# Seven block products for eight in the gate and up projections of a decoder trunk's FFNs, and narrower FFN chunks

## The chip, the core and the metric

The kernel runs on one core of a Trainium2 chip. The metric is the device time in microseconds, the median of the runs shown; smaller is better. TensorE is the matrix engine (PE in the rows; PEld is its weight load), VectorE is DVE, ScalarE is ACT, GpSimd is POOL, and SP issues the DMAs.

## What is computed

One step of a decoder trunk of two layers over 576 tokens: 512 of a prompt and 8 sequences of 8. Each layer has a half-step FFN, a mixer of three gated branches and a second FFN, each behind an RMSNorm with a per-sequence shift and scale. The FFN is what is changed here:

```python
def _swiglu(h, w_gu, w_dn):
    a, b = jnp.split(h @ w_gu, 2, axis=-1)
    return (jax.nn.silu(a) * b) @ w_dn
...
x = x + 0.5 * mod[:, 0, 2][:, None, :] * _swiglu(h, w1_gu, w1_dn)
```

The model width is 1024 (eight blocks of 128), the FFN width 2816 (22 blocks of 128), all in float32. `mod`, the modulation, is `silu(c) @ w_ada + b_ada`, nine vectors of 1024 a layer.

## The kernel before

Everything lies transposed in SBUF: channels on the partitions, tokens along the row. The 576 tokens are two halves of 288 columns (256 of the prompt, 32 of the samples).

**Products.** Every float32 operand is kept as a high and a low part, and a product is three matmuls of 128x128 by 288 columns: low weight by high input (L288), high by low (L290), high by high (L291). `units` (L278) does this for the k blocks of one output tile (128 output channels, one half of the tokens) in one PSUM bank of five, and calls a function that reads the bank. `pair` (L539) runs two output tiles for both halves, 2 x 2 x 8 x 3 = 96 matmuls in a gate or up product.

**Weights.** A raw tile holds 256 output columns of a matrix, 1 MB; SP loads it (L123) into one of two buffers. `Weights.split` (L203) cuts it into slots of 128x1024, a high and a low part each, six slots in all (`NHL`): the high part on ScalarE (L223), the low part, raw less high, on VectorE (L227); every third slot on GpSimd (L221, L225). A slot is cut when an earlier one has had its last use (`done`), so cuts run several tiles ahead of PE.

**FFN.** `ffn` (L548) goes over the width in three chunks of 8, 8 and 6 tiles. Of each chunk it makes gate and up products, two output tiles at a time (`evac_a`, Silu on ScalarE, L556; `evac_b`, the product on VectorE L566 and its two parts on ScalarE L568 and VectorE L569), then the down products over the chunk's tiles, added into `x` (`xupd`, L458). An FFN's first two gate and two up tiles lie in `start_stage` (L479), interleaved with the RMSNorm of the second half of the tokens (`norm3`, L416); the end of a stage (`end_stage`, L509) interleaves the first half's.

**Modulation.** The matmuls for the later modulation vectors are spread as 64 steps over the two FFNs of layer 0, a step every three units; `sched_ada` (L1349) loads each step's four tiles (1 MB) two steps ahead, and `ada_mm` (L319) runs it.

All this is written in program order: each engine's instructions run in the order in which the code issues them, and an engine waits at an instruction until its inputs are there and its output is free.

## Time and profile before

| | before |
|---|---|
| median of three runs | 2694.2 us (2693.83 to 2694.84) |
| span of the profiled execution | 2692.9 us (the page gives no other time of it) |
| TensorE busy (matmuls) | 2668.0 us, 99% |
| TensorE busy (weight loads) | 2581.1 us, 96% |
| VectorE busy | 1043.0 us, 39% |
| ScalarE busy | 631.8 us, 23% |
| GpSimd busy | 603.7 us, 22% |
| read from and written to HBM | 288.02 MB and 3.25 MB |

The page gives each engine's busy time over the whole span. A matmul's record reaches from its start to its modelled end, and matmuls overlap, so the price of one is the distance of two starts. An engine's waits, the chain of work that ended last, and windows of the span tell where its share of idle time lies.

### The profile page before, as it was taken

The numbers are of one execution on the slowest core, as the hardware profiler recorded it, in microseconds if no ns is written. First come the engines' busy times: TensorE is split into PE (matmuls) and PEld (weight loads), VectorE is DVE, ScalarE is ACT, GpSimd is POOL, SyncE is SP. The second block draws the span as 40 slices with busy tenths as digits, with TensorE's granted clock in tenths as the row PEclk, the third lists the DMA queues.
The fourth block names the chain that finished last, engine by engine and source line by source line (L and its number), as shares of the span: only waits on it lengthen the run. The fifth ranks groups of instructions, "written<-read, shape, count | busy, mean of one in ns | idle before, by whom it ended". The sixth has DMA issues, their size and how long they took to land.

```text
span 2692.9 us, 46258 instructions
## 1 busy us (share of the span) xinstructions
PE 2668.0 (99%) x20040; PEld 2581.1 (96%) x20040; DVE 1043.0 (39%) x2094; ACT 631.8 (23%) x1167; POOL 603.7 (22%) x520
## 2 busy tenths in 40 slices
PE   8999999999999999999999999999999999999998
PEld 5999999999999999989999999999999999999998
DVE  5232232643325633223253323237333456232324
ACT  4211112331223321121232122124212233212122
POOL 2111112502133421121142111223020523211111
PEclk9999999999999999999999999999999999999999
DMA  9544542322222254545213222222222232222221
GB/s 287 204 164 166 176 132 69 99 78 79 87 83 83 95 195 165 187 142 172 67 59 110 94 79 79 80 90 85 80 79 93 77 95 68 94 79 85 89 67 56
DMA packets 259689, 294.03 MB, mean 109 GB/s; under 512 B 9996, under 2 KB 223292, under 8 KB 259470
## 3 DMA queue, kind: packets, MB, share of 16 engines
q1 hardware_dynamic: 259486, 291.08, 32.8%
q8 instruction: 158, 2.59, 0.4%
q14 instruction: 45, 0.37, 0.0%
HBM read 288.02 MB, written 3.25 MB: 108 GB/s over the span
## 4 chain that ended last, share of the span: by engine, by line
PE 95%; DVE 2%; DMA 1%; POOL 1%; issue 0%; SPq 0%; ACT 0%; DVEq 0%; POOLq 0%; ACTq 0%
PE mm L288 31%; PE mm L291 30%; PE mm L290 30%; PE adab L326 2%; DVE hlo L436 1%; PE mm L297 1%; DMA adap<-in_w_ada_dram 0%; POOL accsq L373 0%; PE tpb L712 0%; DMA xin<-in_x_prompt_dram 0%; POOL wlo L225 0%; DMA ada<-in_w_ada_dram 0%; DVE u L431 0%; PE nrb L412 0%; DVE us L446 0%
## 5 line engine op out<-in xcount | busy, mean ns | idle before, releaser
L288 PE MATMUL mm<-hhi,wlo 128*128 128x288 f32 x4320 | 1281.7, 298 | 0.0
L291 PE MATMUL mm<-hhi,whi 128*128 128x288 f32 x4320 | 1272.1, 295 | 0.0
L290 PE MATMUL mm<-hlo,whi 128*128 128x288 f32 x4160 | 1229.1, 295 | 0.0
L288 PEld LDWEIGHTS mm<-hhi,wlo 128*128 128x128 f32 x4320 | 810.9, 188 | 34.6 <-issue 33.5
L291 PEld LDWEIGHTS mm<-hhi,whi 128*128 128x128 f32 x4320 | 810.9, 188 | 0.0
L290 PEld LDWEIGHTS mm<-hlo,whi 128*128 128x128 f32 x4160 | 781.1, 188 | 0.3
L227 DVE TENSOR_TENSOR wlo<-raw,whi 128x1024 fp32r<-128x1024 f32 (+1 forms) x277 | 344.3, 1245 | 656.2 <-ACT whi L223 649.2
L221 POOL TENSOR_SCALAR whi<-raw 128x1024 fp32r<-128x1024 f32 (+1 forms) x125 | 131.9, 1055 | 1588.2 <-PE mm L291 1519.0
L288 PE MATMUL mm<-ghi,wlo 128*128 128x288 f32 x1408 | 418.3, 297 | 0.0
L291 PE MATMUL mm<-ghi,whi 128*128 128x288 f32 x1408 | 414.7, 295 | 0.0
L290 PE MATMUL mm<-glo,whi 128*128 128x288 f32 x1408 | 414.5, 294 | 0.0
L223 ACT ACTIVATE whi<-raw 128x1024 fp32r<-128x1024 f32 (+1 forms) x277 | 285.5, 1034 | 517.1 <-PE mm L291 289.5
L225 POOL TENSOR_TENSOR wlo<-raw,whi 128x1024 fp32r<-128x1024 f32 (+1 forms) x125 | 308.9, 2471 | 10.4
L288 PEld LDWEIGHTS mm<-ghi,wlo 128*128 128x128 f32 x1408 | 264.1, 188 | 20.3 <-issue 20.1
L290 PEld LDWEIGHTS mm<-glo,whi 128*128 128x128 f32 x1408 | 264.1, 188 | 0.2
L291 PEld LDWEIGHTS mm<-ghi,whi 128*128 128x128 f32 x1408 | 264.1, 188 | 0.0
L462 DVE SCALAR_TENSOR_TENSOR x<-mm,mod,x 128x256 f32<-128x256 f32 x224 | 108.1, 483 | 321.6 <-PE mm L291 321.5
L568 ACT ACTIVATE ghi<-g 128x288 fp32r<-128x288 f32 x176 | 78.2, 444 | 455.8 <-DVE g L566 455.8
L566 DVE TENSOR_TENSOR g<-mm,sil 128x288 f32<-128x288 f32 x176 | 80.5, 457 | 266.5 <-PE mm L291 265.5
L556 ACT ACTIVATE sil<-mm 128x288 f32<-128x288 f32 x176 | 71.5, 411 | 430.1 <-PE mm L291 404.1
L569 DVE TENSOR_TENSOR glo<-g,ghi 128x288 fp32r<-128x288 f32 x176 | 89.9, 511 | 90.2 <-ACT ghi L568 89.7
L747 ACT ACTIVATE sil<-mm 128x288 f32<-128x288 f32 x96 | 38.8, 409 | 182.4 <-PE mm L291 167.6
(219 smaller groups left out, 1912.8 us busy)
## 6 DMA issues: line engine op xcount, KB each, us to landing
raw<-in_w_gu_dram SPq DMA_DIRECT2D x88, 1024.0 KB
ada<-in_w_ada_dram SPq DMA_DIRECT2D x256, 256.0 KB
raw<-in_w_in_dram SPq DMA_DIRECT2D x48, 1024.0 KB
raw<-in_w_dn_dram SPq DMA_DIRECT2D x32, 1024.0 KB
raw<-in_w_dn_dram SPq DMA_DIRECT2D x16, 768.0 KB
adap<-in_w_ada_dram SPq DMA_DIRECT2D x32, 256.0 KB
raw<-in_w_o_dram SPq DMA_DIRECT2D x8, 1024.0 KB
raw<-in_w_out_b_dram SPq DMA_DIRECT2D x8, 512.0 KB
```

Source lines behind the costliest of these rows:

```text
L221: nc.gpsimd.tensor_scalar(dst_v(hi), src, 1.0, 0.0, ALU.mult, ALU.add)
L223: nc.scalar.activation(dst_v(hi), src, AF.Copy)
L225: nc.gpsimd.tensor_sub(dst_v(lo), src, dst_v(hi).bitcast(F32))
L227: nc.vector.tensor_sub(dst_v(lo), src, dst_v(hi).bitcast(F32))
L288: nc.tensor.matmul(o, wlo, rhi, start=(k == 0), stop=False)
L290: nc.tensor.matmul(o, whi, rlo, start=False, stop=False)
L291: nc.tensor.matmul(o, whi, rhi, start=False, stop=(k == K - 1 and not late))
L462: nc.vector.scalar_tensor_tensor(out=xc, in0=ps[:, :PH], scalar=mod[:, gidx + m, 0:1], in1=xc, op0=ALU.mult, op1=ALU.add)
L556: nc.scalar.activation(t, ps[:, :HALF], AF.Silu)
L566: nc.vector.tensor_mul(g, ps[:, :HALF], sil.pop((j, h)))
L568: nc.scalar.activation(hi, g, AF.Copy)
L569: nc.vector.tensor_sub(glo[j][:, h * HALF:(h + 1) * HALF], g, hi.bitcast(F32))
```

## The change

**Gate and up products by blocks.** For every gate or up pair except an FFN's first, the pair's product is taken as a product of 2 x 2 blocks: the 1024 channels are two halves of four k blocks, the 256 output columns two tiles, the 576 tokens two halves. Seven block products of four k blocks stand for eight, which Strassen's algorithm allows in Winograd's form. It needs four sums of weight blocks (S1 to S4, on GpSimd, in place in the raw tile, L337), four sums of input blocks (T1 to T4, on VectorE, once an FFN, `t_sum` L649, and split by `t_split` L660 and L661), and sums of the products. `Groups.group` runs the seven products in this order: A12·B21 into a bank of its own, copied out by ScalarE (L717); the last product of the group before (`tail`); A11·B11 into the bank `ak`, added to the copy by VectorE (L723); S1·T1, copied out (L731); S2·T2 added on into `ak`, read by VectorE (L736); S4·B22, added by VectorE (L741); S3·T3 added on into `ak`, read by VectorE (L748); and A22·T4 added on into `ak`, deferred as the tail. A product into `ak` waits until the read before it is done. Three of four products of gate and up now go to GpSimd (L912).

**Cuts.** Such a raw tile is cut in eight steps, in the order a, d, S1, S3, c, S2, S4, b: slots a, b and c of 128x1024, d of 128x512, all with the high part on ScalarE (L288) and the low part on VectorE (L290). There are five slots and two half slots for six slots. `pump` runs as many further steps as a place in the group allows.

**Chunks.** The FFN's chunks are 4, 4, 4, 4 and 6 tiles in layer 0, and 4, 6, 6 and 6 in layer 1. The down products of all chunks but the last are added into `x` by three engines (L775, L776, L781).

**Start of an FFN.** The norm (`norm3t`) makes the float32 inputs as tiles of 128x576, which the T sums then overwrite. `start_stage` cuts its third slot behind the normalisation where none is left (`pay`).

**Modulation.** Steps are loaded one step ahead, and their groups go by vectors.

```diff
 NSLOT = 25
-NHL = 6
+NQ = 16
+NB = 5
+NHL = 5
+NHD = 2
+_FEW = ((0, 4), (4, 4), (8, 4), (12, 4), (16, 6))
+_MANY = ((0, 4), (4, 6), (10, 6), (16, 6))
...
+    def add_st(src, c0):
+        def dma(t):
+            nc.sync.dma_start(t.rearrange("p (k c) -> p k c", c=256),
+                              src[:, c0:c0 + 256].rearrange("(k p) c -> p k c", p=P))
+        raws.append((dma, None))
+    def add_ffn(gu, dn, chunks):
+        for f0, nf in chunks:
             for j in range(f0, f0 + nf, 2):
-                add_cols(gu, j * P, KT)
-                add_cols(gu, 2816 + j * P, KT)
+                add = (lambda src, c: add_cols(src, c, KT)) if j == 0 else add_st
+                add(gu, j * P)
+                add(gu, 2816 + j * P)
             for m in range(0, 8, 2):
                 add_cols(dn[f0 * P:(f0 + nf) * P, :], m * P, nf)
...
+                    self.steps += [(r, x) for x in ("a", "d", "S1", "S3", "c", "S2", "S4", "b")]
...
+        def can(self):
+            if self.at >= len(self.steps):
+                return False
+            r, x = self.steps[self.at]
+            if r not in self.rawt:
+                return False
+            if x == "d":
+                return len(self.free["d"]) > 0
+            return x in ("S1", "S2", "S3", "S4") or len(self.free["w"]) > 0
...
+                a11, a12, a21, a22 = first[:, 0], first[:, 1], second[:, 0], second[:, 1]
+                last = x == "b"
+                if x == "d":
+                    hi, lo = self.pair_of(True)
+                    self.cut(hi.rearrange("p (k c) -> p k c", c=P),
+                             lo.rearrange("p (k c) -> p k c", c=P), a22, "AD")
+                    self.slots[-1]["d"] = (hi, lo)
+                    filled = False
+                elif x in ("a", "b", "c"):
+                    hi, lo = self.pair_of(False)
+                    t3 = t.rearrange("p (k c) -> p k c", c=256)
+                    src = t3[:, :, P:256] if x == "c" else t3[:, :, 0:P]
+                    self.cut(hi.rearrange("p (k c) -> p k c", c=P),
+                             lo.rearrange("p (k c) -> p k c", c=P), src, "AD")
+                    if x == "a":
+                        self.slots.append({})
+                    self.slots[-1][x] = (hi, lo)
+                else:
+                    filled = False
+                    o, p, q, op = {"S1": (a22, a21, a22, ALU.add), "S3": (a21, a11, a21, ALU.subtract),
+                                   "S2": (a11, a22, a11, ALU.subtract),
+                                   "S4": (a12, a12, a11, ALU.subtract)}[x]
+                    nc.gpsimd.tensor_tensor(out=o, in0=p, in1=q, op=op)
+            if last:
                 del self.rawt[r]
...
+        def pump(self, n):
+            while n and self.can():
+                self.step()
+                n -= 1
...
+        def need(self, s, x):
+            while x not in s:
+                self.step()
+            return s[x]
...
+    def t_sum(i, q):
+        o, a, b = {1: ((0, q), (1, q), (0, q)), 3: ((1, q), (1, q + 2), (1, q)),
+                   2: ((1, q + 2), (1, q + 2), (0, q)), 4: ((0, q + 2), (0, q + 2), (1, q + 2))}[i]
+        nc.vector.tensor_sub(U[o], U[a], U[b])
...
+        nc.scalar.activation(hi, u3, AF.Copy)
+        nc.vector.tensor_sub(lo, u3, hi.bitcast(F32))
...
+    def t_early():
+        return [lambda i=i, q=q: t_sum(i, q) for i in (1, 3, 2, 4) for q in range(2)] + [
+            lambda i=i, q=q: t_split(i, q) for i in (1, 2, 3) for q in range(2)]
...
+    def blk(i):
+        if isinstance(i, str):
+            k0, h = {"11": (0, 0), "21": (4, 0), "22": (4, 1)}[i]
...
+        def product(self, bank, slot, k0, rhs, start):
+            for k in range(4):
+                whi, wlo = wk(slot, k0 + k)
+                rhi, rlo = rhs(k)
+                o = bank[:, :HALF]
+                nc.tensor.matmul(o, wlo, rhi, start=(start and k == 0), stop=False, skip_group_check=True)
+                nc.tensor.matmul(o, whi, rlo, start=False, stop=False, skip_group_check=True)
+                nc.tensor.matmul(o, whi, rhi, start=False, stop=(k == 3), skip_group_check=True)
...
+        def group(self, evac, m):
+            s = W.take()
+            out = lambda i, h: evac(m + i, h)
+            dk = balloc()
+            self.product(dk, W.need(s, "a"), 4, blk("21"), True)
+            d = qalloc("pd")
+            nc.scalar.activation(d, dk[:, :HALF], AF.Copy)
+            brelease(dk)
+            W.pump(1)
+            self.flush()
+            ak = balloc()
+            self.product(ak, s["a"], 0, blk("11"), True)
+            nc.vector.tensor_add(d, ak[:, :HALF], d)
+            out(0, 0)(d, d)
+            W.give(s["a"])
+            W.pump(1)
+            tick(1)
+            ek = balloc()
+            self.product(ek, W.need(s, "c"), 4, blk(1), True)
+            e = qalloc("pe")
+            nc.scalar.activation(e, ek[:, :HALF], AF.Copy)
+            brelease(ek)
+            W.pump(2)
+            self.product(ak, W.need(s, "b"), 0, blk(2), False)
+            u = qalloc("pu")
+            nc.vector.tensor_add(u, ak[:, :HALF], e)
+            W.pump(1)
+            tick(1)
+            fk = balloc()
+            self.product(fk, s["b"], 4, blk("22"), True)
+            nc.vector.tensor_add(u, fk[:, :HALF], u)
+            brelease(fk)
+            out(0, 1)(u, u)
+            W.give(s["b"])
+            W.pump(1)
+            tick(1)
+            self.product(ak, s["c"], 0, blk(3), False)
+            nc.vector.tensor_add(e, ak[:, :HALF], e)
+            out(1, 1)(e, e)
+            W.give(s["c"])
+            W.pump(1)
+            def tail():
+                self.product(ak, W.need(s, "d"), 0, blk(4), False)
+                out(1, 0)(ak, None)
+                brelease(ak)
+                W.give(s["d"])
+                W.pump(1)
+                tick(1)
+            self.tail = tail
...
+            if late:
+                t = qalloc("xt")
+                nc.scalar.activation(t[:, :PH], ps[:, :PH], AF.Copy, scale=mod[:, gidx + m, 0:1])
+                nc.vector.tensor_mul(
+                    t[:, PH:].rearrange("p (s t) -> p s t", s=4),
+                    ps[:, PH:HALF].rearrange("p (s t) -> p s t", s=4),
+                    mod[:, gidx + m, 1 + 4 * h:5 + 4 * h].unsqueeze(2).to_broadcast([P, 4, 8]))
+                xc = x[:, m, c0:c0 + HALF]
+                nc.gpsimd.tensor_add(xc, xc, t)
...
+        nb = norm_bc(1, nrmbank())
+        late_lo.extend(norm3t(1, l, sub, nb) if st else norm3(1, l, sub, us[0], nb))
+        if W.taken >= len(W.slots):
+            W.pay(None, 1)
         s.append(W.take())
...
+        todo = t_early() if st else []
...
+        units([(s[i], 0, KT, hk(1), evac(i, 1)) for i in (0, 1)], {k: lambda: some(1) for k in range(KT)},
+              True)
...
+                g = sil.pop((j, h))
+                (nc.vector if own is None else nc.gpsimd).tensor_mul(g, ps[:, :HALF], g)
...
-        for f0, nf in ((0, 8), (8, 8), (16, 6)):
+        chunks = CHUNKS[l][sub // 2]
+        for f0, nf in chunks:
...
-                    pair(KT, hk, evac_a, j)
-                    pair(KT, hk, evac_b, j)
+                    G.group(evac_a, j)
+                    G.group(evac_b, j)
...
+            xu = lambda m, h: xupd(m, h, gidx, False, True)
+            if f0 + nf < 22:
+                pair4(nf, grhs, xu, 0, G.flush)
+                for m in range(2, 8, 2):
+                    pair(nf, grhs, xu, m)
...
-    def sched_ada(g0, g1, start, every):
...
-        for n, s in enumerate(steps):
-            def fn(s=s, n=n):
-                ada_mm(s)
-                if n + 2 < len(steps):
-                    ada_fetch(steps[n + 2])
...
+    def sched_ada(groups, start):
+        steps = [(vecs, i, every) for vecs, every in groups for i in range(4 * len(vecs))]
+        ada_fetch(steps[0][:2])
+        at = start
+        for n, (vecs, i, every) in enumerate(steps):
+            def fn(n=n, vecs=vecs, i=i):
+                ada_mm((vecs, i))
+                if n + 1 < len(steps):
+                    ada_fetch(steps[n + 1][:2])
+                if i == 4 * len(vecs) - 1:
+                    after(1, lambda: ada_fin(vecs))
+            after(at, fn)
+            at += every
...
+    after(4, lambda: sched_ada((((2,), 2), ((3, 4), 3), ((5, 6), 3), ((7, 8), 3)), 1))
...
+    after(3, lambda: sched_ada((((9, 10), 3), ((11, 12), 3), ((13, 14), 3), ((15, 16), 3), ((17,), 3)), 2))
```

**VectorE in the gate and up products of layer 1, one pair and the next.** Before; `wlo` is the low part of a weight slot, `g` the product of gate and up, `glo` its low part:

```order
L566 TENSOR_TENSOR g_2113_14981<-mm_14954,sil_14861 128x288
L569 TENSOR_TENSOR glo_14980<-g_2113_14981,ghi_14979 128x288
L566 TENSOR_TENSOR g_2117_15012<-mm_14985,sil_14888 128x288
L569 TENSOR_TENSOR glo_15011<-g_2117_15012,ghi_15010 128x288
L566 TENSOR_TENSOR g_2119_15041<-mm_15016,sil_14915 128x288
L569 TENSOR_TENSOR glo_14980<-g_2119_15041,ghi_14979 128x288
L227 TENSOR_TENSOR wlo_15046<-raw_14834,whi_15045 128x1024
L566 TENSOR_TENSOR g_2123_15074<-mm_15049,sil_14946 128x288
L569 TENSOR_TENSOR glo_15011<-g_2123_15074,ghi_15010 128x288
L227 TENSOR_TENSOR wlo_15079<-raw_14834,whi_15078 128x1024
L227 TENSOR_TENSOR wlo_15197<-raw_14952,whi_15196 128x1024
```

Now; `pd`, `pu`, `pe` are the sums of block products, `dlo` the low part of a half slot:

```order
L290 TENSOR_TENSOR dlo_17503<-raw_17265,dhi_17502 128x512
L723 TENSOR_TENSOR pd_17486<-mm_17506,pd_17486 128x288
L915 TENSOR_TENSOR glo_17521<-pd_17386,ghi_17520 128x288
L290 TENSOR_TENSOR wlo_17543<-raw_17265,whi_17542 128x1024
L736 TENSOR_TENSOR pu_17558<-mm_17506,pe_17539 128x288
L741 TENSOR_TENSOR pu_17558<-mm_17561,pu_17558 128x288
L915 TENSOR_TENSOR glo_17521<-pu_17438,ghi_17520 128x288
L748 TENSOR_TENSOR pe_17539<-mm_17506,pe_17539 128x288
L915 TENSOR_TENSOR glo_17593<-pe_17418,ghi_17592 128x288
L290 TENSOR_TENSOR wlo_17598<-raw_17265,whi_17597 128x1024
L290 TENSOR_TENSOR wlo_17619<-raw_17424,whi_17618 128x1024
L912 TENSOR_TENSOR sil_17500<-mm_17506,sil_17500 128x288
```

Every group, a gate group too, now has four reads of PSUM on VectorE (L723, L736, L741, L748), with low cuts ahead of L723 and L736; before, an up pair had four (L566) and a gate pair none.

**GpSimd at the same place.** Before, whole slots are cut:

```order
L221 TENSOR_SCALAR whi_14948<-raw_14735 128x1024
L225 TENSOR_TENSOR wlo_14949<-raw_14735,whi_14948 128x1024
L221 TENSOR_SCALAR whi_15165<-raw_14952 128x1024
L225 TENSOR_TENSOR wlo_15166<-raw_14952,whi_15165 128x1024
L221 TENSOR_SCALAR whi_15326<-raw_15082 128x1024
L225 TENSOR_TENSOR wlo_15327<-raw_15082,whi_15326 128x1024
```

Now, the weight sums and the products of gate and up take turns (`x4` stands for S1, S3, S2 and S4):

```order
L337 TENSOR_TENSOR raw_17128<-raw_17128 128x4x128 x4
L912 TENSOR_TENSOR pd_17386<-pd_17486,pd_17386 128x288
L337 TENSOR_TENSOR raw_17265<-raw_17265 128x4x128 x3
L912 TENSOR_TENSOR pu_17438<-pu_17558,pu_17438 128x288
L337 TENSOR_TENSOR raw_17265<-raw_17265 128x4x128
L912 TENSOR_TENSOR pe_17418<-pe_17539,pe_17418 128x288
L337 TENSOR_TENSOR raw_17424<-raw_17424 128x4x128 x4
L912 TENSOR_TENSOR pd_17616<-pd_17741,pd_17616 128x288
```

In an up group a product of gate and up stands ahead of S1 and S3 and another ahead of S4; a gate group has the sums alone.

**VectorE at the start of the FFN (1, 0).** Before, the low parts of the normalised input (`hlo`) and the cuts, then the first products:

```order
L436 SCALAR_TENSOR_TENSOR hlo<-u_14613,mod,hhi 128x256 x2
L227 TENSOR_TENSOR wlo_14658<-raw_14150,whi_14657 128x1024
L227 TENSOR_TENSOR wlo_14718<-raw_14264,whi_14717 128x1024
L227 TENSOR_TENSOR wlo_14728<-raw_14661,whi_14727 128x1024
L227 TENSOR_TENSOR wlo_14732<-raw_14661,whi_14731 128x1024
L566 TENSOR_TENSOR g_2085_14762<-mm_14737,sil_14713 128x288
L569 TENSOR_TENSOR glo_14644<-g_2085_14762,ghi_14643 128x288
L566 TENSOR_TENSOR g_2091_14797<-mm_14770,sil_14590 128x288
L569 TENSOR_TENSOR glo_14796<-g_2091_14797,ghi_14795 128x288
```

Now, the last two of eight input sums (`u`), four cuts, and three of six splits (`tlo`):

```order
L649 TENSOR_TENSOR u_15194<-u_15194,u_15343 128x576
L649 TENSOR_TENSOR u_15203<-u_15203,u_15352 128x576
L290 TENSOR_TENSOR wlo_15468<-raw_15136,whi_15467 128x1024
L290 TENSOR_TENSOR dlo_15472<-raw_15136,dhi_15471 128x512
L290 TENSOR_TENSOR wlo_15478<-raw_15136,whi_15477 128x1024
L290 TENSOR_TENSOR wlo_15484<-raw_15136,whi_15483 128x1024
L661 TENSOR_TENSOR tlo_15494<-u_15176,thi_15493 128x576
L661 TENSOR_TENSOR tlo_15501<-u_15185,thi_15500 128x576
L661 TENSOR_TENSOR tlo_15508<-u_15343,thi_15507 128x576
```

All eight sums are ahead of the next tile's cuts, and the six splits stand behind them, ahead of the product that follows (L912).

## Rows read from the trace of the kernel before

**Rows 1.** The page: busy us, share, instructions; 40 slices in tenths, with TensorE's granted clock.

```profile
PE 2668.0 (99%) x20040; PEld 2581.1 (96%) x20040; DVE 1043.0 (39%) x2094; ACT 631.8 (23%) x1167; POOL 603.7 (22%) x520
...
PE   8999999999999999999999999999999999999998
...
PEclk9999999999999999999999999999999999999999
```

**Rows 2.** The page: the chain that ended last, its shares by engine.

```profile
PE 95%; DVE 2%; DMA 1%; POOL 1%; issue 0%; SPq 0%; ACT 0%; DVEq 0%; POOLq 0%; ACTq 0%
```

**Rows 3.** Waits of PE: line, releaser, us in total, times, longest us.

```profile
PE tpb L1244 <- ACT crow L1242: 5.1, 1, 5.1
```

**Rows 4.** Windows of line L288 alone: start to end, length, busy (x count), clock, DMA.

```profile
1420.00:1480.00 60.00, 44.34 (x150) 28.15 (x151) 1.00 0.33 108
1520.00:1580.00 60.00, 44.39 (x151) 28.18 (x151) 1.00 0.26 86
```

**Rows 5.** Groups by line and shape: line, engine, operation, shapes, count; busy us, mean ns.

```profile
L288 PE MATMUL mm<-hhi,wlo 128*128 128x288 f32 x4320 | 1281.7, 298 | 0.0
...
L227 DVE TENSOR_TENSOR wlo<-raw,whi 128x1024 fp32r<-128x1024 f32 x255 | 323.2, 1270 | 601.2 <-ACT whi L223 594.3 <-DMA wrep<-in_w_s_dram 6.5 <-PE tpb L976 0.4
...
L223 ACT ACTIVATE whi<-raw 128x1024 fp32r<-128x1024 f32 x255 | 267.2, 1051 | 511.6 <-PE mm L291 289.5 <-issue 147.1 <-DMA ada<-in_w_ada_dram 35.3
...
L569 DVE TENSOR_TENSOR glo<-g,ghi 128x288 fp32r<-128x288 f32 x176 | 89.9, 511 | 90.2 <-ACT ghi L568 89.7 <-DMA ada<-in_w_ada_dram 0.5
...
L566 DVE TENSOR_TENSOR g<-mm,sil 128x288 f32<-128x288 f32 x176 | 80.5, 457 | 266.5 <-PE mm L291 265.5
...
L568 ACT ACTIVATE ghi<-g 128x288 fp32r<-128x288 f32 x176 | 78.2, 444 | 455.8 <-DVE g L566 455.8
...
L556 ACT ACTIVATE sil<-mm 128x288 f32<-128x288 f32 x176 | 71.5, 411 | 430.1 <-PE mm L291 404.1 <-PE mm L297 25.3 <-PE mm L1285 0.8
...
L431 DVE SCALAR_TENSOR_TENSOR u<-x,mod,nrb 128x256 f32<-128x256 f32 x88 | 37.7, 474 | 7.8 <-PE nrb L412 7.7
...
L763 POOL TENSOR_TENSOR acc<-acc,g 128x288 f32<-128x288 f32 x32 | 25.3, 808 | 151.8 <-DVE g L761 151.8
...
L835 POOL TENSOR_SCALAR cv<-ext,colc 128x512 f32<-128x512 f32 x8 | 12.6, 1580 | 45.6 <-DVE exs L822 45.6
...
L732 DVE TENSOR_TENSOR tg<-tg,u 128x576 f32<-128x576 f32 x8 | 6.1, 758 | 0.3
...
L735 ACT ACTIVATE ybh<-tg 128x576 fp32r<-128x576 f32 x8 | 5.5, 686 | 18.4 <-DVE tg L732 18.4
```

**Rows 6.** Instructions of tile raw: durations in ns (min/median/max), first and last start.

```profile
L227 DVE TENSOR_TENSOR wlo<-raw,whi x277: 957/1226/3414, 29.1 to 2646.5; 128x1024 fp32r<-128x1024 f32 x127, 128x768 fp32r<-128x768 f32 x12
...
L225 POOL TENSOR_TENSOR wlo<-raw,whi x125: 1843/2397/3378, 55.7 to 2649.0; 128x1024 fp32r<-128x1024 f32 x115, 128x768 fp32r<-128x768 f32 x10
...
L123 SPq DMA_DIRECT2D raw<-in_w_gu_dram x88: 367/368/467, 13.7 to 2578.0; - x88
```

**Rows 7.** Windows of all engines at the start of the FFN (1, 0).

```profile
1389.00:1415.00 26.00, 25.71 (x183) 24.64 (x184) 21.94 (x60) 11.28 (x26) 14.38 (x13) 1.00 0.00 1
```

**Rows 8.** Timeline of ScalarE there: start us, us, instruction, count.

```profile
1406.88 2.51 ACT L433 ACTIVATE hhi<-u,mod 128x256 fp32r<-128x256 f32 x6
```

**Rows 9.** The chain that ended last, in order of time: start us, us.

```profile
38.73 7.57 DMA ada<-in_w_ada_dram
```

**Rows 10.** Windows of all engines near the start and at the end.

```profile
15.00:25.00 10.00, 7.66 (x50) 3.65 (x51) 3.60 (x13) 2.58 (x9) 0.66 (x2) 1.00 1.09 359
...
2680.00:2685.00 5.00, 2.37 (x16) 1.81 (x16) 1.87 (x10) 2.94 (x13) 0.20 (x1) 1.00 0.67 236
...
2685.00:2693.00 8.00, 0.00 (x0) 0.00 (x0) 3.03 (x7) 1.95 (x3) 0.85 (x1) 0.68 0.42 148
```

**Rows 11.** Timeline of GpSimd and VectorE at the start of the FFN (1, 0).

```profile
1408.89 2.41 POOL L225 TENSOR_TENSOR wlo<-raw,whi 128x1024 fp32r<-128x1024 f32 x1
...
1409.76 1.86 DVE L569 TENSOR_TENSOR glo<-g,ghi 128x288 fp32r<-128x288 f32 x1 [0.59 <-ACT ghi L568]
```

More of the change, by code (lines that the diff above doesn't have):

```diff
@@ L232, in split, with done @@
                     self.load()
+            return filled
+        def split(self, mode=None):
+            while self.can():
+                if self.step(mode):
+                    return
+        def pump(self, n):
+            while n and self.can():
+                self.step()
+                n -= 1
         def take(self):
+            while self.taken >= len(self.slots):
+                self.step()
             s = self.slots[self.taken]
             self.taken += 1
-            return s
-        def done(self):
+            if isinstance(s, tuple):
+                self.out.append(s)
+            return s
+        def need(self, s, x):
+            while x not in s:
+                self.step()
+            return s[x]
+        def done(self, slot=None):
+            slot = slot or self.out[0]
+            self.out = [o for o in self.out if o is not slot]
+            self.give(slot)
             if self.hold:
@@ L278, in units @@
     def units(specs, hooks={}, late=False):
-        bk = [ps_mm.tile([P, 512], F32, tag="mm", name=nm("mm")) for _ in specs]
+        bk = [balloc() for _ in specs]
         K = specs[0][2]
@@ L501, in start_stage @@
         W.done()
-        units([(s[2], 0, KT, hk(1), evac(2, 1))])
+        units([(s[2], 0, KT, hk(1), evac(2, 1))], {k: lambda: some(1) for k in range(KT)})
         W.done()
         s.append(W.take())
-        for h in range(2):
+        some(99)
+        for h in (1, 0) if st else (0, 1):
             units([(s[3], 0, KT, hk(h), evac(3, h))])
+            if h and st:
+                t_last()
         W.done()
```

335 lines of the change are left out of this document (238 added, 97 removed).

## The prediction

> **What bounds the kernel now.** The page's busy times and slices come first: TensorE is busy 2668.0 of 2692.9 us, in nearly every slice at nine tenths or more, and at the full granted clock throughout, while VectorE, ScalarE and GpSimd are busy 39, 23 and 22% [rows 1]. The chain that ended last is 95% PE [rows 2], and PE's longest wait is one of 5.1 us in the startup [rows 3]. So the bound is the number of matmuls. What one costs is read by counting, since a matmul's own 298 ns are pipelined: in 60 us of gate and up products the line that runs once in three matmuls runs 150 or 151 times [rows 4], which is 0.400 us for three, 0.1333 us for one. A unit of 24 takes 3.2 us, one gate or up pair of output tiles (96) 12.8 us.
>
> The spare time of the other engines is an average. What decides here is how long a chain of them one weight tile needs, against PE's time for that tile.
>
> **Part A, matmuls removed.** 80 pairs of output tiles (10 gate and 10 up in each of four FFNs) go from 8 x 4 x 3 = 96 matmuls to 7 x 4 x 3 = 84. That is 960 x 0.1333 = **-128 us**, all on the path. The bytes of weights stay. Two edits cost nothing while PE's units cover them: 24 more weight loads, of 0.37 us each to issue on SP [rows 6], and the late form of the residual update, which puts one addition of 0.81 on GpSimd into a unit of 1.6 us or more [rows 5]. Without that cover the second would cost up to 0.8 us a unit.
>
> **Part B, the ring of engines in a steady group.** The prices are [rows 5]: ScalarE cuts a slot's high part in 1.05, VectorE the low part in 1.23 when alone (the median of [rows 6]; the mean is drawn up by slow ones), the half slot d by a line between 288 and 1024 columns in 0.63 and 0.69; reads and splits of 288 columns take 0.41 to 0.46, GpSimd's product 0.81. A weight sum of 128x512 on GpSimd has no row. A line through its additions of 288 (0.81) and of 1024 columns (2.40) gives 1.29; the nearest single row, a multiply of 512, is 1.58. I take 1.29, since kind and shape fit, and keep 1.2 to 1.58 for the range.
>
> In program order each engine's queue holds the next engine up. Gate half, in the order in which each waits for the one before: high a 1.05, low a 1.23, VectorE's product for the tail before it 0.46, its split 0.44, high d 0.63, low d 0.69, S1 and S3 2 x 1.29, high c 1.05, low c 1.23, read L736 0.46, the product S3·T3 on PE 12 x 0.1333 + 0.16 for the last matmul's pipeline = 1.76, read L748 0.46, Silu 0.41, high b 1.05, copy L717 0.41: 13.9 us. Up half: high a 1.05, low a 1.23, low d 0.69, read L723 0.46, product 0.81, S1 and S3 2.58, high c 1.05, low c 1.23, reads L736 and L741 0.92, product 0.81, split 0.44 and 0.46, read L748 0.46, product 0.81, split 0.44, high b 1.05, copy L717 0.41: 14.9 us. Hand-offs and the overlap of back-to-back instructions are both below 0.1 us and are set against each other.
>
> Together 28.8 us for two groups in which PE has 168 x 0.1333 = 22.4 us of work: PE waits 6.4 us a pair, where it had 25.6 us of work and no wait. It waits because a later product adds into the same bank that VectorE still has to read, and that read stands behind a low cut, which waits for S3. Each FFN has ten such pairs; its first is priced in C, which leaves 36: 36 x 6.4 = 231 us. At the chunk starts the slots were filled during the down products; in the eight of layer 0, where modulation matmuls also lie between, I give back half a pair's wait, 3.2 us each: **+205 us**. Bounds by the sum's price alone are -14 and +46 us.
>
> **Part C, the first group of an FFN.** New there are eight sums (VectorE) and eight splits of 128x576 (VectorE and ScalarE), priced by rows of that shape at 0.76 and 0.69 [rows 5], in a stretch where VectorE was already busy 21.9 of 26 us [rows 7]. They stand ahead of cuts and reads that PE needs: 16 x 0.76 = 12.2 us, then S1, S3 and the cut of c in series, 2 x 1.29 + 1.05 + 1.23 = 4.9 us: 17 us a start. Three starts give **+51 us**; at the first FFN PE is held to the loads, and I cost it at nothing. The bounds are 0 (all of it beside PE) and 75.
>
> **Part D, the third weight slot of a stage start.** With five slots for six, the third tile is cut only after the normalisation, behind its ScalarE work. That work runs six high parts in 2.52 us [rows 8], 0.42 each. FFN: eight of 0.42, four copies of 0.6 (0.69 less the same overlap of 0.1), a first product of 0.47 [rows 5], then 1.05 + 1.23: 8.5 us with nothing for PE to do. Mixer: eight of 0.42, 0.47, 0.4, 1.05, 1.23: 6.5. Three FFNs and two mixers: **+38 us**; bounds 0 and 50.
>
> **Part E, modulation weights one step ahead.** Of 64 steps (counted in the order of PE's instructions) 26 lie in down parts now. In a chunk of four tiles a unit is 12 x 0.1333 = 1.6 us, a step comes every third, so the load has 4.8 us; the slowest one on the chain took 7.57 [rows 9]. At the 359 GB/s of a full stretch [rows 10] 1 MB takes 2.9 us. So a step costs 0 to 2.8 us, 0 to 72 in all; half, **+36 us**, because down weights share the queue.
>
> **Part F, VectorE beside GpSimd.** A low part of 288 columns that takes 0.46 alone took 1.86 where it began inside a GpSimd cut of 2.41 us, and ended with it [rows 11]. The low cut of c now stands beside S2 and S4. Per group I take half of one sum, 0.65 us, 80 times: **+52 us**, bounds 0 and 103. The Trainium skill's page "SBUF — State Buffer", section "Who interferes with whom", calls the port pair that the two engines share an exclusive lock, which a VectorE instruction with two SBUF inputs contends for. By that rule as an estimate the upper bound would stand in the sum, 2999 us in place of 2948. The row of 1.86 agrees with it; the median of the cuts, 1.23, says that most starts miss.
>
> **Sum.** -128 + 205 + 51 + 38 + 36 + 52 = +254 us. The profiled execution's span of 2692.9 lies 1.3 us under the median of the runs, 2694.2; against that median: **2948 us**. No change that a measurement can tell is 0.2%, 5.4 us.
>
> **The rivals.**
> - *Faster: the cuts stay ahead.* If slots and pools let the next tile's a, S1, S3 and c run while PE is still in the group before, B to F shrink to remnants: 2694 - 128 = 2566, up to 2660 with D and part of E. For it speaks that no engine's own sum in a pair reaches 22.4 us (by the prices above ScalarE about 13, VectorE 15, GpSimd 13); against it, that c's cut needs a slot which the group gives back only at its own last read, and that the queues are in order. It decides at the ring: with C to E as above it must be as short as 22.4 us, without them 26.0 (22.4 + 128/36). Chance 0.09.
> - *Half a ring.* The run-ahead of the chunk starts reaches through the chunk; B halves: 2948 - 103, about 2845. Chance 0.15.
> - *Collisions in full.* Each group waits for a whole sum, and the slower price of 1.58 or E's upper bound may join: 2999 to 3065. For it: the 1.86 row. Against: that median. Chance 0.22.
> - *The clock falls.* Waits of 8 to 12 us at stage starts, and shorter ones throughout, are new. The granted clock is 0.68 in the last 8 us with PE idle, yet 1.00 just before, with PE busy less than half [rows 10]. If the 80 x 84 x 0.1333 = 896 us of group work ran at a mean of 0.9, it would be 100 us more: 3048. The Trainium skill's "TensorE: Matmul & The Clock Gate", section "HAM oscillation — how this bites in real kernels", tells of a kernel that fell to the slower of two clocks in every wait between bursts; the row of 1.00 says that half-idle PE need not. Chance 0.04.
> - *The change doesn't do what it says.* The order of PE's instructions shows seven products a group, so the matmuls are gone; something else would have to give exactly 128 us back: 2694. Chance 0.01.
>
> **How the numbers follow.** The forecast has 0.49, with its own range of 2880 to 2998. Below it come 0.15 at 2845 and 0.09 at 2566 to 2660; above it 0.26 between 2999 and 3065. The range that leaves out the faster case, the upper end of the rest and a little below is 2840 to 3060. Faster by over 0.2%: 0.09. Within: 0.02 (the last rival and the passage between). Slower: 0.89.
>
> **What would show it.** In the profile of the changed kernel PE should be busy some 2540 us, near 86% of its span, with waits of 300 to 400 us. They should stand before L702, released by VectorE's L723, L736 and L748 (B, 200 us or more, 2 to 3 us each, two a group), at three FFN starts two waits of 5 us and more (C), before L422 at five stage starts (D), and before the modulation matmuls, released by DMA (E). Low cuts of L290 should have a mean above 1.3 us (F). GpSimd's L337 should read 1.2 to 1.6. The forecast is wrong if PE stays above 95%, if the waits before L702 end on a weight cut rather than on a read, or if the granted clock drops.

## The result and the profile after

The changed kernel takes 3075.28 us (four runs, 3073.7 to 3078.0) against 2694.45 us: a ratio of 1.1414, interval 1.1398 to 1.143. It is slower by 381 us, where +254 were forecast, and lies just above the range of 2840 to 3060. Its profiled execution spans 3072.8 us, 379.9 more than that of before.

The page of the changed kernel, the lines that answer to [rows 1] and [rows 2]:

```profile
PE 2685.0 (87%) x19084; PEld 2538.3 (83%) x19084; DVE 1339.4 (44%) x2414; ACT 990.7 (32%) x1841; POOL 1189.2 (39%) x1156
...
PE   6988888899999878889787797979999996888877
...
PEclk8999999999999999999998999999999998999999
...
PE 56%; POOL 14%; DVE 12%; ACT 9%; issue 5%; DMA 4%; SPq 0%; POOLq 0%; DVEq 0%; ACTq 0%
```

PE runs 956 instructions fewer (960 matmuls less, four transposes more) and yet is busy 17 us longer. At full clock it would have been busy 2668.0 - 956 x 0.1333 = 2540.6 us. So the 379.9 us are three things: -127.4 of work that went, +362.9 of idle time (3072.8 - 2685.0, against 24.9 before), and +144.4 by which PE is busy longer than its instructions would be at 0.1333 us each.

The mean granted clock is 0.951. In the trace 301 us of the span stand at a clock of 0.50, 190 of them with PE busy; that costs 95 of the 144 us. Two other parts are not the clock. The 512 modulation matmuls are busy 103.0 us where they took 68.2; 7 us of that growth are the low clock, 28 are not. In the step that begins at 1213.78 us, at a clock of 1.00, its eight matmuls start over 2.33 us, one tile's load after the other, where eight whose tiles lie ready start within 0.48 us (1239.72 to 1240.20). And the last matmul before a wait is counted to its modelled end, 0.16 us beyond its price, at 162 waits where before there were 26: some 21 us that are waits too.

The waits of PE, which were one of 5.1 us and small ones [rows 3]:

```profile
PE mm L702 <- DVE pd L723: 128.7, 37, 10.0
PE mm L702 <- DVE pu L736: 82.8, 46, 2.3
PE adab L466 <- DMA ada<-in_w_ada_dram: 43.3, 13, 13.4
PE mm L422 <- DVE wlo L290: 26.3, 4, 9.2
PE mm L702 <- DVE xt L776: 21.5, 7, 4.1
PE mm L702 <- DVE pe L748: 20.4, 25, 3.2
PE mm L702 <- DVE sil L912: 15.7, 3, 6.5
PE mm L422 <- POOL wlo L290: 14.2, 2, 7.6
```

They stand where the forecast put them: before the block products (L702), at stage starts (L422), before the modulation matmuls (L466).

One wait of a gate group in layer 1, in the timelines of GpSimd, ScalarE, VectorE and PE:

```profile
2009.43 6.23 POOL L337 TENSOR_TENSOR raw<-raw 128x512 f32<-128x512 f32 x4 [6.10 <-DVE dlo L290]
...
2012.12 1.06 ACT L288 ACTIVATE whi<-raw 128x1024 fp32r<-128x1024 f32 x1 [1.62 <-POOL raw L337]
...
2013.21 1.31 DVE L290 TENSOR_TENSOR wlo<-raw,whi 128x1024 fp32r<-128x1024 f32 x1 [3.49 <-ACT whi L288]
2014.45 0.45 DVE L736 TENSOR_TENSOR pu<-mm,pe 128x288 f32<-128x288 f32 x1
...
2014.95 0.40 PE L702 MATMUL mm<-thi,wlo 128*128 128x288 f32 x1 [1.73 <-DVE pu L736]
...
2015.32 0.29 PE L704 MATMUL mm<-thi,whi 128*128 128x288 f32 x1
2015.45 0.30 PE L702 MATMUL mm<-thi,wlo 128*128 128x288 f32 x1
...
2016.27 0.44 PE L703 MATMUL mm<-tlo,whi 128*128 128x288 f32 x1
2016.51 0.44 PE L704 MATMUL mm<-thi,whi 128*128 128x288 f32 x1
```

After the second weight sum (2009.43 + 2 x 1.29) ScalarE cuts c's high part, VectorE the low part, and only then comes the read L736, for which PE has waited 1.73 us. VectorE itself had been idle for 3.49 us before that cut. Then the matmuls start 0.13 us apart, and a little later 0.24: the granted clock has fallen to 0.50 (until 2019.0).

### The profile page after: what moved, and what is told of

It reads as the page before. It is cut to its first block, busy times and chain, and to the rows that moved or that the text cites. A ratio compares the mean times of both kernels' runs of the same rounds, so it can differ in the third digit from the quotient of the medians.

```text
span 3072.8 us, 46201 instructions
## 1 busy us (share of the span) xinstructions
PE 2685.0 (87%) x19084; PEld 2538.3 (83%) x19084; DVE 1339.4 (44%) x2414; ACT 990.7 (32%) x1841; POOL 1189.2 (39%) x1156
## 3 DMA queue, kind: packets, MB, share of 16 engines
HBM read 288.02 MB, written 3.25 MB: 95 GB/s over the span
## 4 chain that ended last, share of the span: by engine, by line
PE 56%; POOL 14%; DVE 12%; ACT 9%; issue 5%; DMA 4%; SPq 0%; POOLq 0%; DVEq 0%; ACTq 0%
PE mm L422 14%; PE mm L425 13%; PE mm L424 13%; POOL raw L337 9%; ACT whi L288 6%; DVE wlo L290 5%; PE mm L702 4%; PE mm L703 4%; PE mm L704 4%; DMA ada<-in_w_ada_dram 2%; PE adab L466 2%; POOL x L781 2%; DVE dlo L290 2%; ACT dhi L288 1%; DMA raw<-in_w_dn_dram 1%
## 5 line engine op out<-in xcount | busy, mean ns | idle before, releaser
L290 DVE TENSOR_TENSOR wlo<-raw,whi 128x1024 fp32r<-128x1024 f32 (+2 forms) x437 | 519.5, 1193 | 798.0 <-ACT whi L288 792.7
L288 ACT ACTIVATE whi<-raw 128x1024 fp32r<-128x1024 f32 (+2 forms) x437 | 426.9, 979 | 445.2 <-POOL raw L337 320.8
L422 PE MATMUL mm<-hhi,wlo 128*128 128x288 f32 x1760 | 528.0, 302 | 44.1 <-DVE wlo L290 26.3
L337 POOL TENSOR_TENSOR raw<-raw 128x512 f32<-128x512 f32 x320 | 449.7, 1405 | 292.5 <-DVE dlo L290 253.4
L425 PE MATMUL mm<-hhi,whi 128*128 128x288 f32 x1760 | 521.6, 299 | 0.0
L702 PE MATMUL mm<-thi,wlo 128*128 128x288 f32 x960 | 312.1, 325 | 227.3 <-DVE pd L723 128.7
L424 PE MATMUL mm<-hlo,whi 128*128 128x288 f32 x1600 | 476.8, 298 | 0.0
L422 PE MATMUL mm<-ghi,wlo 128*128 128x288 f32 x1408 | 420.4, 299 | 0.2 <-ACT ghi L914 0.2
L702 PEld LDWEIGHTS mm<-thi,wlo 128*128 128x128 f32 x960 | 194.8, 203 | 262.0 <-DVE pd L723 137.9
L422 PEld LDWEIGHTS mm<-hhi,wlo 128*128 128x128 f32 x1760 | 336.0, 191 | 52.3 <-DVE wlo L290 27.3
L425 PEld LDWEIGHTS mm<-hhi,whi 128*128 128x128 f32 x1760 | 335.8, 191 | 0.0
L702 PE MATMUL mm<-hhi,wlo 128*128 128x288 f32 x960 | 296.2, 309 | 21.5 <-DVE xt L776 21.5
L424 PEld LDWEIGHTS mm<-hlo,whi 128*128 128x128 f32 x1600 | 304.7, 190 | 0.0
L781 POOL TENSOR_TENSOR x<-x,xt 128x288 f32<-128x288 f32 x224 | 210.5, 960 | 235.4 <-DVE xt L776 235.3
L703 PE MATMUL mm<-hlo,whi 128*128 128x288 f32 x960 | 292.2, 304 | 0.0
L704 PE MATMUL mm<-hhi,whi 128*128 128x288 f32 x960 | 291.1, 303 | 0.0
L422 PEld LDWEIGHTS mm<-ghi,wlo 128*128 128x128 f32 x1408 | 265.8, 189 | 21.6 <-issue 15.9
```

The lines of the kernel that those rows point to most:

```text
L288: nc.scalar.activation(hi, src, AF.Copy)
L290: eng.tensor_sub(lo, src, hi.bitcast(F32))
L337: nc.gpsimd.tensor_tensor(out=o, in0=p, in1=q, op=op)
L422: nc.tensor.matmul(o, wlo, rhi, start=(k == 0), stop=False)
L424: nc.tensor.matmul(o, whi, rlo, start=False, stop=False)
L425: nc.tensor.matmul(o, whi, rhi, start=False, stop=(k == K - 1 and not late))
```

## The experiments

**x1: filling PE's waits in the groups.** The edit (and calls with 14 and 11 in a gate group, 0 and 15 in an up group):

```diff
+    def filler(slot, n):
+        nb = ps_1.tile([P, 512], F32, tag="nrm", name=nm("fill"))
+        for k in range(n):
+            nc.tensor.matmul(nb[:, :HALF], wk(slot, k % 8)[0], hhi[:, k % 8, 0:HALF],
...
+            filler(s["c"], fill[0])
             self.product(ak, W.need(s, "b"), 0, blk(2), False)
...
+            filler(s["c"], fill[1])
             self.product(ak, s["c"], 0, blk(3), False)
```

> PE is given extra matmuls into a bank that nothing reads, just before the products that wait: 14 before S2·T2 and 11 before S3·T3 in a gate group, 15 before S3·T3 in an up group, 40 x 40 x 0.1333 = 213 us of extra PE work laid into waits of about the same length. Theory 1 (PE's idle time lets its clock fall, and that is the part of the loss which the forecast left out): the reads come when they came, the granted clock in the groups goes back to 1.00, and the kernel gets faster in spite of the added work, by some 60 to 90 us, to about 2990 to 3015, with PE's mean clock above 0.975. Theory 2 (the matmuls of the groups are slower for another reason, their operands or the adding on in one bank): the clock stays near 0.95 and the time stays at 3075 or grows by up to 60 us where a filler is longer than the wait.

Measured: 3113.35 us, 38 more than the change; mean clock 0.966. Theory 1 in this form fell. The starts of the read that follows A11·B11 show why, first of the changed kernel (L723), then of this one (L729), VectorE's timeline:

```profile
2023.17 0.46 DVE L723 TENSOR_TENSOR pd<-mm,pd 128x288 f32<-128x288 f32 x1
2040.31 0.45 DVE L723 TENSOR_TENSOR pd<-mm,pd 128x288 f32<-128x288 f32 x1
2052.68 0.46 DVE L723 TENSOR_TENSOR pd<-mm,pd 128x288 f32<-128x288 f32 x1
```

```profile
2022.80 0.46 DVE L729 TENSOR_TENSOR pd<-mm,pd 128x288 f32<-128x288 f32 x1
2039.95 0.45 DVE L729 TENSOR_TENSOR pd<-mm,pd 128x288 f32<-128x288 f32 x1
2052.45 0.45 DVE L729 TENSOR_TENSOR pd<-mm,pd 128x288 f32<-128x288 f32 x1
```

Two groups take 29.5 us and 29.6 us: in a steady pair the other engines set the pace. The time lies in theory 2's range, but its reason fell too, for through the filled pair the granted clock is 1.00. What a low clock costs in the changed kernel depends on where it falls. The longer half of a pair, from an up group's read L723 to the next gate group's, takes 17.1 us at a clock of 0.90 (1860.52 to 1877.64) and at 1.00 (2023.17 to 2040.31): there the loss lies inside a wait. The shorter half does not hide it, as windows of all engines show:

```profile
2009.27:2023.17 13.90, 11.66 (x74) 11.43 (x75) 6.07 (x9) 5.93 (x10) 6.00 (x4) 0.88 0.16 48
2040.31:2052.68 12.37, 10.14 (x74) 9.90 (x75) 5.91 (x8) 5.08 (x9) 8.68 (x6) 1.00 0.04 14
```

Three of the twelve shorter halves of steady pairs in layer 1 are such slow ones; with the fillers none is. The 38 us are fillers in groups that wait less: the half behind a change of chunk, 12.5 us (1848.01 to 1860.52), takes 14.0 with them, and some halves of layer 0, where modulation matmuls fill the time anyway, 15.6 in place of 12.3.

**x2: the weight sums left out.**

```diff
-                    nc.gpsimd.tensor_tensor(out=o, in0=p, in1=q, op=op)
+                    pass
```

> The four weight sums S1 to S4 on GpSimd are left out, so the block products use unsummed weights; all else stands in the same order. Theory 1 (a ring of queues in which the low cut of c stands behind S1 and S3, and reads stand behind that cut): the ring loses 2 x 2.58 us a pair, so most of the 6.2 us a pair that PE waits go, and with them most of the slow clock: 2750 to 2830 us, waits before L702 under 110 us in place of 248. Theory 3 (VectorE's own work and its collisions with GpSimd's products hold the reads up, not the sums): waits before L702 stay over 180 us, and the time over 2930.

Measured: 2810.72 us, in the range of theory 1. Waits before L702 released by these reads are 84 us in all, most of it in two rows:

```profile
PE mm L702 <- DVE pd L723: 58.1, 25, 7.6
...
PE mm L702 <- DVE pe L748: 18.9, 25, 3.1
```

The sums are in the ring. That alone does not tell whether there are too many of them or whether they stand in the wrong place.

**x3: plain products, the rest of the change kept.**

```diff
-                    G.group(evac_a, j)
-                    G.group(evac_b, j)
+                    pair(KT, hk, evac_a, j)
+                    pair(KT, hk, evac_b, j)
```

(The raw tiles are cut whole, and the input sums are left out.)

> Gate and up products go back to eight plain products a pair, and the sums of inputs and weights with them; the narrower chunks, five slots, the fetch one step ahead and the three-engine update of x stay. Theory 1: no waits in the groups, 960 matmuls more than the change; left are the third slot (about 40 us) and the modulation loads (20 to 43 us), and little for the clock: 2755 to 2790 us. Rival (the narrow chunks and the update on three engines cost much themselves): over 2830.

Measured: 2792.08 us, 98 above the kernel before; 2 us above the upper end. Its idle time is 87.3 us (2789.1 - 2701.8), 62 more than before, and PE is busy 33 us longer than at 0.1333 us an instruction (2701.8 against 2668.0 + 4 x 0.1333), 18 of them by the low clock. So the starts and the modulation loads cost about 98 us, and the blocks the other 283, net of the matmuls that they save.

```profile
PE mm L422 <- DVE wlo L290: 28.1, 4, 9.2
PE adab L466 <- DMA ada<-in_w_ada_dram: 13.4, 6, 8.0
PE mm L422 <- POOL wlo L290: 13.2, 2, 6.6
```

**x4: filling the waits at stage starts**, in x3's kernel:

```diff
+        fb = balloc("fill")
+        for k in range(45):
+            nc.tensor.matmul(fb[:, :HALF], wk(s[0], k % 8)[0], hk(0)(k % 8)[0], start=True, stop=True,
...
         if W.taken >= len(W.slots):
```

> As x3_plain, with 45 extra matmuls (6.0 us, into a bank that nothing reads) at each of the five stage starts, where PE waits 6.6 to 9.2 us for the cut of the third slot. Nothing that the kernel needs is moved. Theory 1 (a wait lets PE's clock fall, and the matmuls after it pay about 2 us): PE's mean clock rises above 0.990, and the time falls by 6 to 12 us, to 2780 to 2786. Theory 2 (the slow matmuls after a wait have another cause): within 2 us of 2792.

Measured: 2786.17 us (2782.34 to 2791.13), 5.9 less than x3, whose runs lie between 2790.8 and 2793.3; the clock goes from 0.988 to 0.995, and the low clock costs PE 9.9 us in place of 18.4. The fall is just short of the 6 to 12 us that were expected, and the runs' ranges touch, so the time alone would not settle it. The clock does: in x3 it falls at all five starts, here at two of the three that still have 3.2 us of the wait. Here PE is what all others wait for, so it counts.

**x5: the update of x back on VectorE.**

```diff
-            xu = lambda m, h: xupd(m, h, gidx, False, True)
+            xu = lambda m, h: xupd(m, h, gidx, False, False)
```

> The update of x after the down products goes back to VectorE (three instructions a unit, as in the kernel before); ScalarE and GpSimd lose their part of it, GpSimd 224 additions of 0.96 us. Theory 1 (at a chunk's start PE waits because the first weight sums stand behind these additions in GpSimd's queue): the 8 to 14 us that a change of chunk costs above its products in layer 1 fall to under 6, and the kernel takes 2990 to 3035 us. Rival (the first group's cuts on ScalarE and VectorE hold it up, whatever GpSimd does): VectorE has more to do, and the time is 3065 or more.

Measured: 3032.07 us, 43 less, or 3 us at each of 14 changes of chunk. In layer 1 they still cost 9 us (four tiles) and 5 to 7 us (six) above their products. The late update of x is a part of the wait, a third; most six-tile changes came under 6 us, as theory 1 has it, the four-tile ones did not. ScalarE's part of the update went as well, and PE's waits for it (L776, 21.5 us) became 7.6, so the run does not tell GpSimd's queue from ScalarE's.

**x6: the order of the queues.** The core of the edit; `POINTS` says for seven places of a group what is issued there (p: a step of the cuts, m: an output's product, h: its split):

```diff
+POINTS = ['ph', 'mpmm', 'mh', 'hpp', '', 'hpppmp', '']
...
-                    self.steps += [(r, x) for x in ("a", "d", "S1", "S3", "c", "S2", "S4", "b")]
+                    self.steps += [(r, x) for x in ('a', 'd', 'S1', 'S2', 'S3', 'S4', 'c', 'b')]
...
             nc.vector.tensor_add(d, ak[:, :HALF], d)
-            out(0, 0)(d, d)
+            self.outs += [(out(0, 0), d, d)]
             W.give(s["a"])
-            W.pump(1)
+            self.point(1)
```

> The same instructions in another order: the four weight sums of a tile run in a row before the cut of c, that cut and b's move behind the reads L741 and L748, and the products and splits of an output are issued one or two reads later. No instruction, slot or bank is added or left out. Theory 1 (the order of the queues makes the ring, no engine is short of time: ScalarE 13, VectorE 15, GpSimd 13 of 22.4 us a pair): waits before L702 fall from 248 to under 150 us and the kernel takes 2850 to 2920 us. Theory 3 (the engines' work and their collisions are too much for 22.4 us): above 3000.

(S2 here overwrites an operand of S3 before its use, so the weights differ from the kernel's, with the same instructions; x9 has the right order.) Measured: 2887.09 us, 188 less, as theory 1 has it. VectorE's timeline, the read after A11·B11 in a steady pair, and the head of PE's waits:

```profile
1782.40 0.44 DVE L756 TENSOR_TENSOR pd<-mm,pd 128x288 f32<-128x288 f32 x1
1792.77 0.46 DVE L756 TENSOR_TENSOR pd<-mm,pd 128x288 f32<-128x288 f32 x1
1804.73 0.44 DVE L756 TENSOR_TENSOR pd<-mm,pd 128x288 f32<-128x288 f32 x1
```

```profile
PE mm L731 <- DVE pd L756: 108.6, 19, 11.1
```

A steady pair now takes 22.3 us, PE's own 22.4. No engine was short of time there; the order in the queues made the wait. What is left are 19 long waits, at starts of FFNs and chunks. The low cuts of a whole slot have a mean of 1.342 us in this run, more than the 1.278 of the change, and no steady pair waits for them.

**x9: no early cuts at the end of the down products**, with the sums in the right order:

```diff
                 for m in range(2, 8, 2):
+                    W.hold = m in HOLDM
                     pair(nf, grhs, xu, m)
+                W.hold = False
+                W.owed = 0
```

(`HOLDM` is 6, the last pair of down products.)

> As x6_order, with the sums in the order S1, S3, S2, S4, and with the last pair of down products of a chunk cutting no further slots, so that its reads of PSUM and the copies of the first group do not stand behind a cut that waits for the second tile's sums. Nothing is added or left out. Theory 1 (at a chunk's start too the wait is one of order: a cut that is early in the queue waits for sums that are late): a change of chunk in layer 1 falls from about 6 to 10 us above its products to under 3, and the kernel takes 2810 to 2845 us. Rival (the down part gives GpSimd and VectorE more than they can do): within 15 us of 2887.

Measured: 2811.81 us, 75 less than x6. A change of chunk of six tiles in layer 1, the read after A11·B11 before and behind it, first in the changed kernel, then here (VectorE's timelines):

```profile
1789.81 0.45 DVE L723 TENSOR_TENSOR pd<-mm,pd 128x288 f32<-128x288 f32 x1
...
1848.01 0.45 DVE L723 TENSOR_TENSOR pd<-mm,pd 128x288 f32<-128x288 f32 x1
```

```profile
1757.29 0.46 DVE L757 TENSOR_TENSOR pd<-mm,pd 128x288 f32<-128x288 f32 x1 [0.87 <-PE mm L734]
...
1807.49 0.45 DVE L757 TENSOR_TENSOR pd<-mm,pd 128x288 f32<-128x288 f32 x1
```

58.2 us against 50.2, with (288 + 84) x 0.1333 = 49.6 us of matmuls between. The cut of the second tile's c stood in ScalarE's and VectorE's queues ahead of the reads of the last down products and of the first group, and waited for that tile's sums. Five of the six changes of layer 1 come under 3 us, one of the four-tile ones has 4.2. In x6 as here all four sums stand ahead of the cut of c; what their order is worth by itself was not run.

**x8: all of it together**, with a sixth slot (`NHL = 6`, `NQ = 10`), the gate pair after an FFN's first by plain products, which gives the input sums 12.8 us more, products and updates on VectorE, and the modulation steps spaced by 3.25 units, a down unit counting 0.6. The lines that set these:

```diff
-NQ = 16
-NHL = 5
+NQ = 10
+NHL = 6
+EV = 3.25
+NPL = 1
...
-                add = (lambda src, c: add_cols(src, c, KT)) if j == 0 else add_st
+                    if j == 0 or (j == 2 and part < NPL):
+                        add_cols(gu, col, KT)
...
-        tick(len(specs))
+        tick(len(specs) * (0.6 if NOTICK else 1))
```

> The seven products with all the waits that the runs have named taken out by order and space: order and hold as in x9_order_hold, a sixth slot (the small tiles are 10 in place of 16), the gate pair after an FFN's first by plain products (12 matmuls an FFN more, time for the input sums), the products of gate and up on VectorE, the update of x on VectorE, and the modulation steps spaced by 3.25 units, of which a down unit counts 0.6. Theory 1: PE's waits fall to under 70 us, the clock stays at 0.99 or more, and the time is 2694 - 128 + 6 and what is left of the waits, 2590 to 2640 us: faster than both kernels. Theory 3 (the seven products need more of VectorE and GpSimd than there is): 2694 or more.

Measured: 2629.92 us, a ratio of 0.9764 to the kernel before, interval 0.975 to 0.9777: 2.4% faster than it and 14% faster than the change.

```profile
PE 2570.8 (98%) x19132; PEld 2465.7 (94%) x19132; DVE 1503.7 (57%) x2952; ACT 884.3 (34%) x1595; POOL 893.0 (34%) x808
...
PE   7999999999999999999999999999999999999998
...
PEclk9999999999999999999999999999999999999999
```

PE idles 56 us, and the low clock costs 7. VectorE is busier than in any other kernel here. Beyond what is listed, `POINTS` differs from x9's in two places and the input sums are issued at other units. What each of its edits beyond x9 is worth was not run apart.

## Why the prediction was wrong

The direction and the place of the waits were right; the size was not: the sum of +254 fell short by 127 us. **The steps that failed are the clock, which the sum put at nothing and which slowed PE by 95 us, and part E, "half", which had 36 us where 71 came.** All other waits (B, C, D and F) grew by 341 us, the modelled ends counted in, where 346 stood. So 95 + 35 - 5 = 125 of the 127 us have a place.

*Bound, and part A.* Right: PE was full, and 127 us of its work went.

*Part B, the ring in a steady group.* Right: 28.8 us were worked out for a pair, 29.5 to 29.6 measured, and up to 31.0 where the clock falls in the shorter half. The sum's price of 1.29, taken between rows, has a median of 1.287 (the tile view of the changed kernel). The bounds of -14 and +46 were taken for 40 pairs; for the 36 of the term they are -13 and +42. That the ring is one of order was shown by x6. The rival "the cuts stay ahead" named the point from which it decides, 22.4 us; x6 gets there.

*Part B, the starts of chunks.* "I give back half a pair's wait" failed too, by less. The slots were cut early, as assumed, but early cuts stood in the queues ahead of reads that PE needs. The change of chunk that stands under x9, in the changed kernel:

```profile
1838.58 4.52 POOL L781 TENSOR_TENSOR x<-x,xt 128x288 f32<-128x288 f32 x4 [2.53 <-DVE xt L776]
1843.06 6.15 POOL L337 TENSOR_TENSOR raw<-raw 128x512 f32<-128x512 f32 x4
...
1845.69 1.06 ACT L288 ACTIVATE whi<-raw 128x1024 fp32r<-128x1024 f32 x1 [5.63 <-POOL raw L337]
...
1846.78 1.30 DVE L290 TENSOR_TENSOR wlo<-raw,whi 128x1024 fp32r<-128x1024 f32 x1 [5.08 <-ACT whi L288]
...
1848.51 0.61 PE L702 MATMUL mm<-thi,wlo 128*128 128x288 f32 x1 [6.49 <-DVE pd L723]
```

GpSimd adds four updates of x before it starts the second tile's sums; ScalarE's cut of that tile's c waits 5.63 us for them, the low cut follows, and only then comes the read L723 (1848.01). Counted between reads L723, the six changes of chunk in layer 1 take 12.0, 8.6, 7.2, 14.1, 7.8 and 10.1 us above their products, 10 in the mean, where the same half of a steady pair takes 5.9. By PE's waits alone, modelled ends counted in, a pair at a change has 9.2 us in layer 1, where the sum had 7.7 with part F, and 6.1 in the eight of layer 0, beside the modulation loads, where it had 4.5: 22 us too little over the fourteen. The 22 steady pairs have 122 us where 169 stood, so the waits in the groups were not what the sum lacked. x9 took 75 us back by holding the cuts, and x5 43 by moving the update.

*Part C.* Two waits at each of three starts, 4.0 and 10.0, 6.5 and 9.8, 5.3 and 9.8: 45 us for 51. *Part D.* 26.3 + 14.2 us of waits before L422, 40.5 for 38.

*Part E.* **This step failed.** The waits are 43.3 us, but the modulation matmuls hold 28 more that show as busy time, since within a step, too, PE waits for the next tile. Together that is 71 us, just under the upper bound of the part, 72.

*Part F.* The steady pair of 29.6 us lies between the ring of 28.8 and the 30.1 that it has with 1.3 for collisions. One collision stands in the ring:

```profile
1868.86 1.28 POOL L337 TENSOR_TENSOR raw<-raw 128x512 f32<-128x512 f32 x1
...
1869.41 1.04 DVE L915 TENSOR_TENSOR glo<-pu,ghi 128x288 fp32r<-128x288 f32 x1 [1.40 <-ACT ghi L914]
1870.38 0.45 DVE L748 TENSOR_TENSOR pe<-mm,pe 128x288 f32<-128x288 f32 x1
```

A split that takes 0.46 alone takes 1.04 beside a sum, ahead of the read L748: 0.6 us a pair, about half of the term. The forecast's own sign for this part, low cuts with a mean above 1.3 us, did not come (1.278 for whole slots), and x6 ran with longer cuts and no wait in its steady pairs. Of the rival "collisions in full" E's upper bound came, a whole sum's wait in each group did not.

*The clock.* **This step failed: the sum had no term for it.** It was a rival at 0.04, though the forecast named a drop of the granted clock among the signs of being wrong. All waits together were forecast at 382 us (205 + 51 + 38 + 36 + 52), and the idle time grew by 363. Beyond that, PE was busy 144 us longer than its matmuls' price, 2685 us where the forecast's own signs had some 2540; 95 of them are the low clock. Some 14 of the 95 lie in the longer halves of eight steady pairs, where they take the place of a wait. The rival's price of 100 us is near that partly by luck: it was worked out for the groups alone, and 29 of the 95 us lie outside them, at starts of stages and of the kernel. At the start of the FFN (1, 0), the windows of all engines:

```profile
1620.00:1636.00 16.00, 16.00 (x121) 15.78 (x119) 10.57 (x14) 3.62 (x6) 6.03 (x4) 1.00 0.20 67
1636.00:1642.00 6.00, 0.01 (x1) 0.00 (x0) 5.29 (x8) 4.12 (x7) 0.00 (x0) 0.85 0.26 87
1642.00:1656.00 14.00, 3.73 (x14) 3.41 (x15) 7.45 (x12) 5.83 (x11) 5.72 (x4) 0.50 0.00 0
1656.00:1665.00 9.00, 9.00 (x54) 9.00 (x53) 3.20 (x5) 3.09 (x6) 2.18 (x3) 0.74 0.19 60
```

PE idles, the granted clock goes to 0.50 (1.2 of 2.4 GHz), and in the last window 54 matmuls take the time of 67. The row of the kernel before that spoke against this, a clock of 1.00 with PE half busy [rows 10], was one stretch of 5 us and did not bear it. The Trainium skill's page "TensorE: Matmul & The Clock Gate", section "What's actually happening", says that the clock passes at one of two ratios, a half or the whole; the spacing of 0.24 us after 0.13 agrees.

The waits and the clock are not simply added. In the longer half of a steady pair the low clock costs nothing, since PE would wait anyway; in the shorter half, and after a wait at a start, where PE sets the time (x3 and x4), it does. How much of the 95 us would come back at full clock and with the waits left as they are was not measured. What was: where waits went, the slow time went with them.

| kernel | PE idle, us | PE busy over price, us | of that by the low clock, us |
|---|---|---|---|
| before | 25 | 0 | 0 |
| x8 | 56 | 24 | 7 |
| x4 | 59 | 27 | 10 |
| x3 | 87 | 33 | 18 |
| x2 | 179 | 87 | 43 |
| x9 | 191 | 77 | 44 |
| x1 | 246 | 109 | 63 |
| x6 | 246 | 102 | 71 |
| x5 | 353 | 138 | 90 |
| the change | 388 | 144 | 95 |

(Idle is the span less PE's busy time; over price is PE's busy time less 2668.0 and 0.1333 us for each instruction more or less than 20040; by the low clock is half of the busy time at a granted clock of 0.50.) Beyond the 25 us of before, a microsecond of idle time comes with 0.24 us (x8) to 0.32 us (x6) at the low clock. The 363 idle us and the 144 of busy time are the 507 us by which the changed kernel is longer than its matmuls.

## What to carry to other kernels

When TensorE's work is cut, add up the other engines' steps along the queues, not their busy shares: a cut that is issued early but waits long holds up every urgent read behind it, in steady groups (x6, 188 us) and where one stage turns into the next (x9, 75 us). Put what PE waits for ahead of what only the next tile needs, and issue a step when its inputs are there; here that was worth 264 us (x9) with no instruction added. A forecast that adds waits to a kernel whose PE was always busy needs a term for the clock, here 0.24 to 0.32 us for each us of waiting, and a load that comes in pieces can cost more than the idle time shows.
